# First layer's MLP: latents by a seven-product scheme, context as its own stage, rotation tables in double batches on two engines

## The chip, the cores and the metric

One core of one Trainium2 chip runs the whole program. The metric is the device time of one execution in microseconds; three runs of the kernel before took 3078.25, 3080.51 and 3085.92 us, so its time is the median, 3080.51 us. TensorE multiplies matrices into PSUM; VectorE, ScalarE and GpSimd work element by element; SyncE (SP) issues most of the DMAs, GpSimd's queue a few.

## The reference

Two layers over 1024 latent tokens and 256 context tokens of width 1024. The first layer mixes by attention, the second by a state-space model, and each ends in an MLP with hidden width 4096. Only the first layer's MLP treats the context too, since the context is not needed after the second mixer.

```
def _mlp(h, w1, w2):
    return jnp.square(jax.nn.relu(h @ w1)) @ w2

for i in range(DEPTH):                       # DEPTH = 2
    need_ctx = i < DEPTH - 1
    ...                                      # modulation, mixer
    x = x + g1 * y
    h2 = _rmsnorm(x, norm2_g[i], NORM_EPS) * (1.0 + sc2) + sh2
    x = x + g2 * _mlp(h2, mlp_w1[i], mlp_w2[i])
    if need_ctx:
        ctx = ctx + g1c * yc
        h2c = _rmsnorm(ctx, norm2_g[i], NORM_EPS) * (1.0 + sc2c) + sh2c
        ctx = ctx + g2c * _mlp(h2c, mlp_w1[i], mlp_w2[i])
return _rmsnorm(x, final_g, NORM_EPS)
```

## The kernel before

Everything is kept transposed: 128 channels on the partitions, tokens along the free axis, in blocks of 512, 512 (latents) and 256 tokens (context). Matrices are multiplied in a rounded 32-bit format, and for accuracy each operand is split into a high and a low part: a product is three matmuls, high by high, high by low and low by high (`mm3`, lines 328 to 335).

Stages follow one another: modulation and input projection; attention; output projection (`out_proj`, line 1118), which also forms the statistics and the normed, split input `Hh`, `Hl` of the MLP; the first MLP (`mlp`, line 1142); the state-space mixer (`ssm`, line 1627); its gate (`glu`); the second MLP (`mlp_s`, line 1187).

`mlp` goes through the 4096 hidden channels in 16 steps of 256. In each step one call of `weights` (line 317) brings two pages of the first matrix and another two of the second: a page of 512 KB is loaded into one of two raw buffers, ScalarE makes its high part (line 324), VectorE its low part (line 325), and the raw buffer is then free for the next page. Two buffers hold high and two hold low parts. Then come, for context and both latent blocks, 48 matmuls of the first product, relu and square (lines 1158 to 1161), 48 matmuls of the second product and the additions to the residual stream (`add_x`, line 1109). A pair of pages so serves 144 matmuls.

Between these, `prep` takes one step of a side job at a time (`work` in `build`): the second layer's modulation (`ada`, line 262: 12 chunks of 4 pages, each page multiplied by TensorE as it comes, and one transposition a chunk) and the rotation tables of the state-space mixer (`ssm_table`, line 1556): for each of 32 channel pairs, a table of 160 complex powers is doubled eight times over by complex products on GpSimd, and stored to memory.

`mlp_s` computes the second layer's MLP by Strassen's scheme: the operands are cut into 2 x 2 blocks, and seven products of block sums take the place of eight. Its eight units alternate between the first and the second matrix, each with seven products of 48 matmuls of 512 columns; sums of weight blocks are made by DMAs that add into memory, sums of inputs by VectorE. Its order is written out: every operation is given to a planner (`Plan`, line 115) with an engine, a cost and a due time, and the planner's order is then fixed for TensorE, ScalarE, VectorE and GpSimd.

Elsewhere only GpSimd keeps the order of the program; on the other engines and on SP's queue a scheduler orders by the program's order and by when it reckons an operation to be ready. Every engine, and each queue, executes its list in order: an instruction that waits holds all behind it.

After the first MLP, `u_norm` (line 1576) forms the statistics of the stream and copies it to memory for the mixer.

Of the kernel before, what the change touches and what calls it, by code (L numbers as in the profile page):

```python
# [30 lines left out]
def host_layout(inp):  # L31
# [26 lines left out]
    a["w1b"] = g["mlp_w1"][1].reshape(2, 4, P, 4, 2, 512).transpose(3, 4, 0, 2, 1, 5).reshape(4, 2, 2, P, 2048)  # L58
    a["w2b"] = g["mlp_w2"][1].reshape(4, 2, 4, P, 2, 512).transpose(0, 4, 1, 3, 2, 5).reshape(4, 2, 2, P, 2048)
# [157 lines left out]
class Net:  # L217
    def __init__(self, tc, a):
        self.tc, self.nc, self.a = tc, tc.nc, a

# [107 lines left out]
    def mm3(self, out, terms, first=True, last=True):  # L328

        nc = self.nc  # L330
        n = len(terms)
        for i, (lh, ll, rh, rl) in enumerate(terms):
            nc.tensor.matmul(out, lh, rh, start=first and i == 0, stop=False)  # L333
            nc.tensor.matmul(out, lh, rl, start=False, stop=False)  # L334
            nc.tensor.matmul(out, ll, rh, start=False, stop=last and i == n - 1)  # L335


    def rstd_steps(self, xv, n, ps, sp, then, spread=True, added=0):
# [57 lines left out]
        bc = ps.tile([P, 512], F32, name="n_bc", tag="bc", bufs=1)  # L396
# [78 lines left out]
    def in_proj(self, ps, sm, xs, pools, prep):  # L475
# [27 lines left out]
        pools()  # L503
# [614 lines left out]
    def out_proj(self, ps, sp):  # L1118
        nc, a = self.nc, self.a

        def then(b, bc):
            self.scaled(lambda ct: self.xv0(ct, b), BLK[b][1], 0, 1, int(b == 2), bc, sp, self.to_H(b))
        step = self.follow(self.xv0, ps, sp, then, added=5)
        w = {}
        for b in (2, 0, 1):
            n = BLK[b][1]

            for mp in range(4) if b else (2, 3, 0, 1):
# [4 lines left out]
                for j in range(2):  # L1133
# [5 lines left out]
                    step(b, ct)  # L1139
        step()  # L1140

    def mlp(self, i, first, xv, ps, mp, prep, last):

        nc, a = self.nc, self.a
        for f in range(16):
            w1 = self.weights(a["w1"][2 * f:2 * f + 2])
            w2 = self.weights(a["w2"][2 * f:2 * f + 2])
            hid = {}
            for b in first:
                n = BLK[b][1]  # L1150
                hh = mp.tile([P, 2, n], F32R, name="hid_h", tag=f"hh{b}", bufs=1)
                hl = mp.tile([P, 2, n], F32R, name="hid_l", tag=f"hl{b}", bufs=1)
                for j in range(2):
                    acc = ps.tile([P, 512], F32, name="m_acc", tag="mm")
                    wh, wl = (x[:, j].rearrange("p (k m) -> p k m", k=KT) for x in w1)
                    self.mm3(acc[:, :n], [(wh[:, k], wl[:, k], self.Hh[b][:, k], self.Hl[b][:, k]) for k in range(KT)])
                    r = mp.tile([P, 512], F32, name="m_r", tag="m_r", bufs=2)
                    nc.scalar.activation(r[:, :n], acc[:, :n], AF.Relu)  # L1158
                    nc.scalar.activation(hh[:, j], r[:, :n], AF.Square)  # L1159
                    nc.vector.tensor_tensor(r[:, :n], r[:, :n], r[:, :n], ALU.mult)  # L1160
                    nc.vector.tensor_tensor(hl[:, j], r[:, :n], hh[:, j].bitcast(F32), ALU.subtract)
                prep()
                hid[b] = hh, hl
            step = last() if f == 15 else lambda b, ct: ct % 4 or prep()
            for b in sorted(first):
                n = BLK[b][1]
                hh, hl = hid[b]
                for ct in range(KT):
                    acc = ps.tile([P, 512], F32, name="m_acc", tag="mm")
                    c = slice(P * ct, P * ct + P)  # L1170
                    self.mm3(acc[:, :n], [(w2[0][:, j, c], w2[1][:, j, c], hh[:, j], hl[:, j]) for j in range(2)])
                    self.add_x(xv(ct, b), acc[:, :n], self.mv(i, 5, ct, int(b == 2)))
                    step(b, ct)
        step()


# [10 lines left out]
    def mlp_s(self, mp, wp, ps):  # L1187
        nc, a = self.nc, self.a
        V, S, PE, G = nc.vector, nc.scalar, nc.tensor, nc.gpsimd

        blocks = []
        blocks += [wp.tile([P, 4, 512], F32, name=f"st_wa{j}") for j in range(2)]
        sa = [wp.tile([P, 2, 2, 512], F32R, name=f"st_a{j}") for j in range(2)]
        blocks += [wp.tile([P, 4, 512], F32, name=f"st_wb{j}") for j in range(2)]
        sb = [wp.tile([P, 2, 512], F32R, name=f"st_b{j}") for j in range(4)]

        blocks.append(self.xc.rearrange("p k s c -> p (k s c)").rearrange("p (k c) -> p k c", k=4))
        hid = {(m, n): mp.tile([P, 4, 512], F32, name=f"st_h{m}{n}") for m in range(2) for n in range(2)}

        t1, t2, t4, tt = (mp.tile([P, 4, 512], F32, name=f"st_t{x}") for x in ("1", "2", "4", "t"))  # L1200
        bank = [ps.tile([P, 4, 512], F32, name=f"st_b{i}") for i in range(2)]
        rings = dict(A=[(f"A{i}",) for i in range(5)], a=[(f"a{i}",) for i in range(2)], b=[(f"b{i}",) for i in range(4)], X0=[("X0",)], X1=[("X1",)])
# [6 lines left out]
        xv = lambda m, n, t: self.xv1(4 * m + t, n).rearrange("p s c -> p (s c)")  # L1209
        gate = lambda m, t: self.mv(1, 5, 4 * m + t, 0)  # L1210
# [634 lines left out]
def build(tc, a, probe=None):  # L1845
# [14 lines left out]
    with ExitStack() as es:  # L1860
        net.setup(es)
        with net.pool("H0") as hp, ExitStack() as ws:
# [27 lines left out]
            with net.pool("ps2", 5, space=PSUM) as ps, tc.manual_schedule(engines={mybir.EngineType.Pool}):  # L1890
                with net.pool("nrm") as sp:
                    net.out_proj(ps, sp)
                if stop("out_proj"):
                    return
# [59 lines left out]
```

## Time and profile before

| what | value |
|---|---|
| runs | 3078.25, 3080.51, 3085.92 us |
| profiled execution | 3081.73 us |
| its span | 3080.0 us |
| TensorE busy | 93% of the span |
| VectorE busy | 62% |
| ScalarE busy | 38% |
| GpSimd busy | 38% |

The profile comes from one execution of its own. The span runs from the first to the last instruction that the profile shows. Matmuls are pipelined: the duration of one overlaps the next, so the pace of a row of matmuls is the distance between their starts. PEclk is the granted clock of TensorE as a share of 2.4 GHz. "A <- B" in a tile's name reads "A is written from B".

### The profile page before, as it was taken

Reading aid. Unit: us, or ns where it says so; the run is one execution under the profiler, and the core shown is the slowest. Engines: PE = TensorE matmul, PEld = TensorE weight load, DVE = VectorE, ACT = ScalarE, POOL = GpSimd, SP = SyncE. Lnnn points to the kernel's source line nnn. Section 1 sums busy time; section 2 is a strip of 40 time slices with the busy share of each in tenths; the row PEclk is TensorE's granted clock in tenths of the full one; section 3 lists DMA queues with packets and bytes.
Section 4 is the critical chain, followed back from the end, with each engine's and each line's share of the span. In section 5 each row is a group of like instructions: output and inputs, shape, how many; then the busy total and the mean of one; then the engine's idle time right before and its main releaser. Section 6 shows DMA issues by size and latency. Waiting matters only on the chain. (4 is left out here: it accounts for less than half of the span.)

```text
span 3080.0 us, 46255 instructions
## 1 busy us (share of the span) xinstructions
PE 2878.7 (93%) x17352; PEld 2377.3 (77%) x17352; DVE 1920.8 (62%) x3337; ACT 1185.0 (38%) x2211; POOL 1160.0 (38%) x2346
## 2 busy tenths in 40 slices
PE   7999998888999999999999999967699799999997
PEld 4878887777878777787888888856588688888885
DVE  3887686988664555554554545489923566666665
ACT  3322214676663321111112121245422365656563
POOL 3343233555442277777787000167623200000001
PEclk9999999999999999999999999988899899999998
DMA  6356664233543124333311111366432444554441
GB/s 241 110 187 220 206 221 143 70 90 104 154 118 140 55 97 128 108 120 101 76 60 48 44 41 42 101 184 182 125 108 75 111 117 126 125 126 125 125 110 55
DMA packets 172305, 363.47 MB, mean 118 GB/s; under 512 B 34689, under 2 KB 97185, under 8 KB 162865
## 3 DMA queue, kind: packets, MB, share of 16 engines
q1 hardware_dynamic: 162384, 310.62, 31.5%
q0 software_dynamic: 9696, 49.90, 7.5%
q8 instruction: 136, 2.23, 0.3%
q14 instruction: 89, 0.72, 0.1%
HBM read 294.97 MB, written 65.49 MB: 117 GB/s over the span
## 5 line engine op out<-in xcount | busy, mean ns | idle before, releaser
L1316 PE MATMUL st_b<-st_b,st_a 128*128 128x512 f32 x2688 | 614.2, 391 | 10.3 <-DVE st_b L1307 7.2
L1316 PEld LDWEIGHTS st_b<-st_b,st_a 128*128 128x128 f32 x2688 | 506.7, 189 | 117.8 <-DVE st_b L1307 7.8
L324 ACT ACTIVATE w_hi<-w_raw 128x1024 fp32r<-128x1024 f32 x132 | 136.7, 1053 | 460.6 <-PE m_acc L334 351.7
L333 PE MATMUL m_acc<-hid_h,w_hi 128*128 128x512 f32 (+1 forms) x768 | 277.1, 361 | 0.0
L333 PE MATMUL m_acc<-Hh,w_hi 128*128 128x512 f32 (+1 forms) x768 | 273.9, 357 | 0.0
L334 PE MATMUL m_acc<-hid_l,w_hi 128*128 128x512 f32 (+1 forms) x768 | 272.6, 355 | 0.0
L335 PE MATMUL m_acc<-Hh,w_lo 128*128 128x512 f32 (+1 forms) x768 | 272.3, 354 | 0.0
L335 PE MATMUL m_acc<-hid_h,w_lo 128*128 128x512 f32 (+1 forms) x768 | 272.1, 354 | 0.0
L334 PE MATMUL m_acc<-Hl,w_hi 128*128 128x512 f32 (+1 forms) x768 | 272.1, 354 | 0.0
L325 DVE TENSOR_TENSOR w_lo<-w_raw,w_hi 128x1024 fp32r<-128x1024 f32 x132 | 169.3, 1294 | 155.7 <-ACT w_hi L324 148.2
L1109 DVE SCALAR_TENSOR_TENSOR xl<-m_acc,m,xl 128x512 f32<-128x512 f32 x256 | 189.5, 747 | 116.4 <-PE m_acc L335 116.1
L1160 DVE TENSOR_TENSOR m_r<-m_r 128x512 f32<-128x512 f32 (+1 forms) x96 | 60.8, 635 | 229.0 <-ACT hid_h L1159 228.8
L333 PEld LDWEIGHTS m_acc<-hid_h,w_hi 128*128 128x128 f32 x768 | 145.0, 189 | 36.0 <-issue 14.4
L333 PEld LDWEIGHTS m_acc<-Hh,w_hi 128*128 128x128 f32 x768 | 145.7, 190 | 24.4 <-issue 4.5
L334 PEld LDWEIGHTS m_acc<-hid_l,w_hi 128*128 128x128 f32 x768 | 145.1, 189 | 22.9 <-issue 3.4
L335 PEld LDWEIGHTS m_acc<-Hh,w_lo 128*128 128x128 f32 x768 | 145.7, 190 | 20.3
L335 PEld LDWEIGHTS m_acc<-hid_h,w_lo 128*128 128x128 f32 x768 | 145.1, 189 | 20.6
L334 PEld LDWEIGHTS m_acc<-Hl,w_hi 128*128 128x128 f32 x768 | 145.7, 190 | 19.2
L1158 ACT ACTIVATE m_r<-m_acc 128x512 f32<-128x512 f32 (+1 forms) x96 | 50.1, 524 | 254.9 <-PE m_acc L335 254.0
L333 PE MATMUL ip_acc<-Hh,w_hi 128*128 128x512 f32 (+1 forms) x384 | 143.1, 374 | 4.1 <-ACT Hh L471 4.1
L334 PE MATMUL ip_acc<-Hl,w_hi 128*128 128x512 f32 (+1 forms) x384 | 139.3, 363 | 1.5 <-DVE Hl L472 1.2
L335 PE MATMUL ip_acc<-Hh,w_lo 128*128 128x512 f32 (+1 forms) x384 | 138.6, 362 | 0.0
(399 smaller groups left out, 6753.7 us busy)
## 6 DMA issues: line engine op xcount, KB each, us to landing
ada_raw<-in_wada_dram SPq DMA_DIRECT2D x96, 512.0 KB, 4.2
w_raw<-in_w_dram SPq DMA_DIRECT2D x64, 512.0 KB, 4.2
s_par<-pD SPq DMA_DIRECT2D x32, 864.0 KB, 4.5
at_q<-qD SPq DMA_DIRECT2D x152, 128.0 KB, 2.7
w_raw<-in_win_dram SPq DMA_DIRECT2D x24, 512.0 KB, 4.6
pD<-tb_cs POOLq DMA_DIRECT2D x32, 320.0 KB, 2.5
pD<-sl_w SPq DMA_DIRECT2D x16, 576.0 KB, 3.4
st_wa<-in_w1b_dram SPq DMA_DIRECT2D x9, 1024.0 KB, 6.3
```

Source lines behind the costliest of these rows:

```text
L324: nc.scalar.activation(hi[:, j], r, AF.Copy)
L325: nc.vector.tensor_tensor(lo[:, j], r, hi[:, j].bitcast(F32), ALU.subtract)
L333: nc.tensor.matmul(out, lh, rh, start=first and i == 0, stop=False)
L334: nc.tensor.matmul(out, lh, rl, start=False, stop=False)
L335: nc.tensor.matmul(out, ll, rh, start=False, stop=last and i == n - 1)
L1109: nc.vector.scalar_tensor_tensor(xv, av, gate, xv, op0=ALU.mult, op1=ALU.add)
L1158: nc.scalar.activation(r[:, :n], acc[:, :n], AF.Relu)
L1160: nc.vector.tensor_tensor(r[:, :n], r[:, :n], r[:, :n], ALU.mult)
L1316: PE.matmul(bk[p][:, mt], x, y, start=(p in (1, 2, 5) and t == 0 and i == 0), stop=(t == 3 and i == 2), skip_group_check=True)
```

## The change

The first layer's latents go through `mlp_s`, which now takes its tiles as arguments; `mlp0` and `mlp1` are its two callers. The context has a stage `mlp_ctx` before it, in two halves of 2048 hidden channels: first all 16 chunks of the hidden layer, then the second product into four PSUM banks over eight pairs of pages, and the additions at the end. The weights of the first layer are thus read twice, once as pages and once as blocks. The modulation and the tables are stepped by `prep` in the output projection (24 times) and the context stage (64 times). The latents' normed input is kept unsplit (`Hr`) and made after the output projection. In `mlp_s` two input sums share one tile and are formed again in later units; the second layer has six weight buffers in place of five, and the last statistics are stepped earlier.

```
-    def mm3(self, out, terms, first=True, last=True):
+    def mm3(self, out, terms, first=True, last=True, check=True):
...
+        def scaled(b, bc, **put):
+            self.scaled(lambda ct: self.xv0(ct, b), BLK[b][1], 0, 1, int(b == 2), bc, sp, **put)
         def then(b, bc):
-            self.scaled(lambda ct: self.xv0(ct, b), BLK[b][1], 0, 1, int(b == 2), bc, sp, self.to_H(b))
+            if b == 2:
+                scaled(b, bc, put=self.to_H(b))
+            else:
+                rs[b] = bc
...
+        def norms():
+            for b in range(2):
+                scaled(b, rs[b], to=lambda ct: self.Hr[b][:, ct])
+        return norms
...
+    def mlp_ctx(self, ps, mp, prep):
...
+        for f in range(2):
+            hid = []
+            for q in range(8):
+                w1 = self.weights(a["w1"][16 * f + 2 * q:16 * f + 2 * q + 2])
                 for j in range(2):
+                    acc = ps.tile([P, 512], F32, name="c_acc", tag="mm")
                     wh, wl = (x[:, j].rearrange("p (k m) -> p k m", k=KT) for x in w1)
+                    self.mm3(acc[:, :n], [(wh[:, k], wl[:, k], H[:, k], L[:, k]) for k in range(KT)])
+                    hh, hl = (mp.tile([P, n], F32R, name=f"c_{x}", tag=f"c_{x}{2 * q + j}", bufs=1) for x in "hl")
+                    r = mp.tile([P, n], F32, name="c_r", tag="c_r", bufs=2)
+                    nc.scalar.activation(r, acc[:, :n], AF.Relu)
+                    nc.scalar.activation(hh, r, AF.Square)
+                    nc.vector.tensor_tensor(r, r, r, ALU.mult)
+                    nc.vector.tensor_tensor(hl, r, hh.bitcast(F32), ALU.subtract)
+                    hid.append((hh, hl))
+                    prep()
+            acc = [ps.tile([P, 512], F32, name="c_acc", tag="mm") for _ in range(4)]
+            for q in range(8):
+                w2 = self.weights(a["w2"][16 * f + 2 * q:16 * f + 2 * q + 2])
                 for ct in range(KT):
...
+                        ins = self.mm3(o, [(w2[0][:, j, c], w2[1][:, j, c], *hid[2 * q + j]) for j in range(2)], first=q == 0 and ct % 2 == 0, last=q == 7, check=False)
...
+                    if ct % 4 == 3:
+                        prep()
+            for ct in range(KT):
+                self.add_x(self.xv0(ct, b), acc[ct // 2][:, n * (ct % 2):n * (ct % 2) + n], self.mv(0, 5, ct, 1))
...
+                    if p == 6 and (second or u == 0):
+                        made["t1", t] = plan.add("V", 0.66, r - 14, F(tt_, V, tt[t], b12[t], b11[t], ALU.subtract), [hd(0, 1, t), hd(0, 0, t)] if second else [])
...
+                    elif p == 5 and not second and u:
+                        made["t1", t] = plan.add("V", 0.66, r - 14, F(tt_, V, tt[t], t2[:, t], b22[t], ALU.add))
+                    if p == 4:
+                        made["t4", t] = plan.add("V", 0.66, r - 13, F(tt_, V, z4[t], b21[t], z2[t], ALU.add), [made.get(("t2", t)), halves[2, t, "b"], *([] if second else [halves[5, t, "b"]])])
...
+                    for j, fn in enumerate(tail_steps[p == 4]):
+                        tail = plan.add("S", 0.6, e + 4 + 0.6 * j, fn, [*x, made["x", 4, j] if p == 4 else None, tail])
...
+    def mlp0(self, mp, ps, step, sp, banks):
+        blocks = [mp.tile([P, 4, 512], F32, name=f"st_w{j}") for j in range(4)] + [self.xc.rearrange("p k s c -> p (k s c)").rearrange("p (k c) -> p k c", k=4)]
...
+        self.mlp_s(0, self.xv0, self.Hr, blocks, sa, sb, hid, t2, tt, bank,
+                   self.tail(step))
...
-    def ssm_table(self, pair, pz):
...
+    def ssm_tables(self, pz):
+        nc, V, G = self.nc, self.nc.vector, self.nc.gpsimd
+        for b in range(16):
+            ep = pz.tile([P, 2, 2, 2, 8], F32, name="tb_ep", tag="tb_ep", bufs=2)
+            nc.sync.dma_start(ep.rearrange("p a d r n -> p a (d r n)"), self.eD[:, 2 * b:2 * b + 2].rearrange("p a d r n -> p a (d r n)"))
+            cs = pz.tile([P, 2, 2, 2, 160], F32, name="tb_cs", tag="tb_cs", bufs=1)
...
+            for q in range(8):
+                n = 1 << q
+                w = min(n, 160 - n)
+                mr, mi = (ep[:, :, :, r, q:q + 1].broadcast_to([P, 2, 2, w]) for r in range(2))
+                x, y = (cs[:, :, r, :, :w] for r in range(2))
+                for e, o, u, v, k, op in ((G, cs[:, :, 0, :, n:n + w], x, y, 0, ALU.subtract), (V, cs[:, :, 1, :, n:n + w], y, x, 1, ALU.add)):
+                    e.tensor_tensor(o, mr, u, ALU.mult)
+                    e.tensor_tensor(t[k][:, :, :, :w], mi, v, ALU.mult)
+                    e.tensor_tensor(o, o, t[k][:, :, :, :w], op)
+                if q % 2:
+                    yield
+            nc.gpsimd.dma_start(self.pD[:, 2 * b:2 * b + 2, 1088:1728], cs.rearrange("p a r d k -> p a (r d k)"))
...
+                with net.pool("nrm", side="right") as sp:
+                    norms = net.out_proj(ps, sp, prep)
+                    hs.close()
+                    hr = hs.enter_context(net.pool("hr0"))
+                    net.Hr = [hr.tile([P, KT, 512], F32, name=f"hr{b}") for b in range(2)]
+                    norms()
+                with net.pool("ctx") as mp, net.pool("nrm1", side="right") as sp:
+                    net.mlp_ctx(ps, mp, prep)
+                    for g in (ada, tables):
+                        for _ in g:
+                            pass
...
+                    step = net.u_norm(rp, sp, banks)
+                    for ct in range(KT):
+                        step(2, ct)
+                    step()
+            net.bc_bufs = 1
+            with net.pool("mlp0") as mp, net.pool("ps6", space=PSUM) as ps:
+                net.mlp0(mp, ps, step, sp, banks)
```

## Rows read from the trace of the kernel before

**Rows 1.** The page's busy times: engine, busy us, share of the span, instructions.
```profile
PE 2878.7 (93%) x17352; PEld 2377.3 (77%) x17352; DVE 1920.8 (62%) x3337; ACT 1185.0 (38%) x2211; POOL 1160.0 (38%) x2346
```

**Rows 2.** By stretch: length, busy PE, PEld, DVE, ACT, POOL; clock, DMA share, GB/s.
```profile
1060.70:2001.50 940.80, 939.67 (x5136) 776.31 (x5136) 470.93 (x708) 189.23 (x302) 503.75 (x1684) 1.00 0.25 80
2411.00:2430.30 19.30, 5.79 (x28) 3.94 (x26) 9.04 (x17) 5.79 (x9) 9.13 (x9) 0.64 0.00 0
2430.00:3047.60 617.60, 614.24 (x2696) 506.51 (x2696) 424.75 (x570) 365.17 (x578) 30.68 (x34) 0.99 0.46 116
```

**Rows 3.** Matmul groups by form: count, busy us, mean ns, idle before.
```profile
L1316 PE MATMUL st_b<-st_b,st_a 128*128 128x512 f32 x2688 | 614.2, 391 | 10.3 <-DVE st_b L1307 7.2 <-ACT st_a L1292 2.5 <-DVE st_a L1295 0.5
L333 PE MATMUL m_acc<-Hh,w_hi 128*128 128x512 f32 x512 | 200.9, 392 | 0.0
L333 PE MATMUL m_acc<-Hh,w_hi 128*128 128x256 f32 x256 | 73.0, 285 | 0.0
```

**Rows 4.** TensorE's timeline in the first MLP: start us, duration us, what.
```profile
1075.07 0.39 PE L333 MATMUL m_acc<-Hh,w_hi 128*128 128x512 f32 x1
...
1082.55 0.39 PE L333 MATMUL m_acc<-Hh,w_hi 128*128 128x512 f32 x1
...
1097.16 0.64 PE L285 MATMUL ada_acc<-ada_raw,act 128*32 128x256 f32 x8
...
1127.76 0.28 PE L333 MATMUL m_acc<-Hh,w_hi 128*128 128x256 f32 x1
...
1133.16 0.28 PE L333 MATMUL m_acc<-Hh,w_hi 128*128 128x256 f32 x1
```

**Rows 5.** SP's queue at the start of the second layer's gate.
```profile
2231.37 0.33 SPq L323 DMA_DIRECT2D w_raw<-in_glua_dram  x1
2232.57 0.33 SPq L323 DMA_DIRECT2D w_raw<-in_glub_dram  x1
2237.38 0.33 SPq L323 DMA_DIRECT2D w_raw<-in_glua_dram  x1
2239.49 0.33 SPq L323 DMA_DIRECT2D w_raw<-in_glub_dram  x1
```

**Rows 6.** VectorE's groups by form, 1060 to 2003 us.
```profile
L325 DVE TENSOR_TENSOR w_lo<-w_raw,w_hi 128x1024 fp32r<-128x1024 f32 x62 | 76.0, 1247 | 57.2 <-ACT w_hi L324 57.1
L1160 DVE TENSOR_TENSOR m_r<-m_r 128x256 f32<-128x256 f32 x32 | 13.9, 436 | 33.8 <-ACT hid_h L1159 33.8
L293 DVE TENSOR_TENSOR ada_e<-ada_e 64x512 f32<-64x512 f32 x12 | 8.4, 698 | 8.0 <-ACT ada_e L291 7.9
L447 DVE TENSOR_TENSOR rs_t<-rs_y 128x4 f32<-128x4 f32 x3 | 0.5, 160 | 1.4 <-POOL rs_y L441 1.4
```

**Rows 7.** GpSimd: the tables by stretch, groups by form, the tables' store.
```profile
1060.00:1960.00 900.00, 467.24 (x1632) 1.00 0.24 76
...
L1382 POOL TENSOR_TENSOR tb_cs<-tb_ep,tb_cs 128x2 f32<-128x2 f32 x32 | 7.7, 240 | 83.9 <-DMA tb_ep<-eD 83.9
L1384 POOL TENSOR_TENSOR tb_cs<-tb_cs,tb_t 128x128 f32<-128x128 f32 x32 | 19.6, 612 | 2.5
L1718 POOL TENSOR_TENSOR s_ab<-s_ab,s_ab 128x320 f32<-128x320 f32 x32 | 36.6, 1144 | 23.2 <-DVE s_ab L1713 22.7
...
pD<-tb_cs POOLq DMA_DIRECT2D x32, 320.0 KB, 2.5
```

**Rows 8.** Timeline of TensorE and ScalarE at three joints of stages.
```profile
1070.25 0.41 PE L333 MATMUL m_acc<-Hh,w_hi 128*128 128x256 f32 x1
...
1071.32 0.41 PE L335 MATMUL m_acc<-Hh,w_lo 128*128 128x256 f32 x1
...
2020.32 4.29 PE L1706 MATMUL s_X<-s_U,s_par 128*64 128x160 f32 x48 [5.07 <-ACT s_U L1669]
...
3058.36 2.19 ACT L367 ACTIVATE st_t<-xl 128x512 f32<-128x512 f32 x4 [2.08 <-PE st_b L352]
```

**Rows 9.** By stretch, behind a norm's broadcast; columns as in rows 2.
```profile
1069.90:1071.40 1.50, 1.50 (x9) 1.50 (x9) 1.12 (x2) 0.00 (x0) 0.33 (x1) 0.50 0.00 0
```

More of the change, by code (lines that the diff above doesn't have):

```diff
@@ L1 @@
+from contextlib import nullcontext
 from functools import partial as F
@@ L326, in weights @@
         return hi, lo
-    def mm3(self, out, terms, first=True, last=True):
-        nc = self.nc
-        n = len(terms)
+    def mm3(self, out, terms, first=True, last=True, check=True):
+        mm = F(self.nc.tensor.matmul, **({} if check else dict(skip_group_check=True)))
+        n, ins = len(terms), None
         for i, (lh, ll, rh, rl) in enumerate(terms):
-            nc.tensor.matmul(out, lh, rh, start=first and i == 0, stop=False)
-            nc.tensor.matmul(out, lh, rl, start=False, stop=False)
-            nc.tensor.matmul(out, ll, rh, start=False, stop=last and i == n - 1)
+            x = mm(out, lh, rh, start=first and i == 0, stop=False)
+            ins = ins or x
+            mm(out, lh, rl, start=False, stop=False)
+            mm(out, ll, rh, start=False, stop=last and i == n - 1)
+        return ins
     def rstd_steps(self, xv, n, ps, sp, then, spread=True, added=0):
@@ L395, in rstd_steps @@
             return
[L396 removed]
+        bc = ps.tile([P, 512], F32, name="n_bc", tag="bc", bufs=self.bc_bufs)
         for j in range(nb):
@@ L1363, in mlp_s @@
                 if last and p in (3, 4):
[L1365 to L1368 removed]
+                    x = [made["x", q, t] for q in (2, 7, 3) for t in range(4)]
+                    for j, fn in enumerate(tail_steps[p == 4]):
+                        tail = plan.add("S", 0.6, e + 4 + 0.6 * j, fn, [*x, made["x", 4, j] if p == 4 else None, tail])
             base += 28 * PK
@@ L1374, in mlp_s, with shim, tail @@
                 s["fn"]()
-            step()
-        self.plan = plan
+            tail_steps[2]()
+    def shim(self, sq, bank, **views):
+        small = {x: [self.act[:, 2 * i + j, 0:8] for j in range(2)] for i, x in enumerate(("n_v", "n_r", "rs_y", "rs_t"))}
+        return Views(None, n_sq=sq, **small, **views), bank is not None and Views(None, st=[bank[:, t] for t in range(2)], bc=[bank[:, t] for t in range(2, 4)])
+    def tail(self, step):
+        return [F(step, 1, ct) for ct in (4, 5, 6, 7, 0, 1, 2, 3)] + [F(step, 0, ct) for ct in range(4)], [F(step, 0, ct) for ct in range(4, 8)], step
@@ L1861, in build @@
         net.setup(es)
-        with net.pool("H0") as hp, ExitStack() as ws:
-            H(hp, range(3))
+        with ExitStack() as ws:
+            weight_pools(ws)
+            hc, hs = ws.enter_context(net.pool("Hc")), ws.enter_context(ExitStack())
+            hp = hs.enter_context(net.pool("H0"))
+            for x in "hl":
+                setattr(net, "H" + x, [(hc if b == 2 else hp).tile([P, KT, BLK[b][1]], F32R, name=f"H{x}{b}") for b in range(3)])
             with net.pool("ps0", 5, space=PSUM) as ps, net.pool("small", side="right") as sm:
@@ new lines, in build, with prep @@
+            rp = es.enter_context(net.pool("rms", side="right"))
+            net.bc_bufs = 2
+            with net.pool("ps2", 4, space=PSUM) as ps, tc.manual_schedule(engines={mybir.EngineType.Pool}), ExitStack() as ts:
+                ap, tp = (ts.enter_context(net.pool(x, side="right")) for x in ("ada", "tables"))
+                ada = net.ada([(1, n) for n in range(12)], ps, ap, ap, 2)
+                tables = net.ssm_tables(tp)
+                def prep():
+                    next(ada, None)
+                    next(tables, None)
+                with net.pool("nrm", side="right") as sp:
+                    norms = net.out_proj(ps, sp, prep)
+                    if stop("out_proj"):
+                        return
+                    hs.close()
[6 more added lines that the diff above has]
+                        for _ in g:
+                            pass
+                    net.ada_gain(1, 0)
+                    net.ada_gain(1, 1)
+                    sp, banks = Views(sp), Views(ps)
+                    step = net.u_norm(rp, sp, banks)
+                    for ct in range(KT):
+                        step(2, ct)
+                    step()
```

189 lines of the change are left out of this document (66 added, 123 removed).

## The prediction

> **What bounds the kernel now.** I read the page's busy times first, then the busy time by stretch, then the matmul groups by form, then the timeline at the places where a stage begins or ends. TensorE is busy 2878.7 us of a span of 3080.0 us [rows 1], and the first layer's MLP is its purest stretch: from 1060.7 to 2001.5 us, 939.67 of 940.80 us busy at a granted clock of 1.00, while VectorE works 470.93 us and ScalarE 189.23 us [rows 2]. There the time is the number of matmuls times the distance between their starts, and nothing else. Durations in the groups overlap (a 512-column matmul reads 392 ns), so I take distances: eleven triples of 512 columns between 1075.07 and 1082.55 us give 7.48 / 33 = 0.227 us each; fifteen triples of 256 columns between 1127.76 and 1133.16 us give 5.40 / 45 = 0.120 us each [rows 4]. Six groups of 512 matmuls of 512 columns and six of 256 matmuls of 256 columns (one of each in [rows 3]) are 3072 x 0.227 + 1536 x 0.120 = 697 + 184 = 881 us. The rest of the 940.8 us is mostly the modulation's 48 page steps, 0.64 us each [rows 4].
>
> **The change part by part.** The sum is made against the profiled execution: 3081.73 us, of which 3080.0 us is span. The median of the runs is 3080.51 us, 1.2 us lower.
>
> *Latents by Strassen.* The second layer's MLP multiplies matrices of the same size and needs 2688 matmuls of 512 columns [rows 3]; it stays fed, with 614.24 of 617.60 us busy [rows 2]. The first layer's latents drop from 3072 to 2688: 384 x 0.227 = **-87.0 us**. The new stage's splits, block sums by DMA and residual adds are those that lie beside the second layer's matmuls; I cost them at nothing as long as TensorE stays near 99% there. The second layer loses two kept sums and forms them again in three of its eight units, 24 VectorE operations of 0.68 us. That is 16 us on an engine with 424.75 of 617.60 us busy [rows 2], hidden behind matmuls: 0, at worst +3 where a sum comes late.
>
> *Context as a stage of its own.* Its 1536 matmuls of 256 columns remain: 0 in matmul time. What goes is cover. Before, a pair of weight pages fed 144 matmuls; now it feeds 48, which last 48 x 0.120 = 5.76 us. There are two raw buffers, and a page's buffer is reloaded only when VectorE has split it. The gate stage of the second layer shows one turn undisturbed (load, high part, low part): a load issued at 2231.37, the next into the same buffer at 2237.38 us, 6.0 us; the other buffer took 2232.57 to 2239.49, 6.9 us [rows 5]. A pair needs both buffers, so the loop gives a pair every 6.0 to 6.9 us. While modulation steps remain (37 of 61, after 24 in the output projection, so some 18 pairs with two each), TensorE itself takes 5.76 + 2 x 0.64 = 7.0 us and the loop hides. For the other 14 pairs I take 6.5 us, between the two turns: 14 x 0.74 = **+10 us**. Bounds: 0 if loads run ahead, +28 if shared transfers add another 1.3 us a pair.
>
> *Tables on two engines.* On GpSimd alone they took 467.24 us over the MLP's 900 us [rows 7], idle capacity that nobody waited for. Now sixteen double batches must fit into the output projection and the first 40 steps of the context stage, and VectorE works in the chain. A batch on GpSimd is three operations at each of eight widths of 4 to 256 elements. From 0.24 us at the smallest and 0.61 at 128 elements, and for 256 an estimate of 0.95 between that and 1.14 us at 320, these make 10 us, plus 0.6 us for the store's issue and some 3 us until its one buffer is free again (2.5 us to landing at half the bytes [rows 7]): 14 us a batch. VectorE's half is about 5.8 us, an estimate between 0.16 us at 4 and 0.44 at 256 elements [rows 6]. In the context stage ten batches want 140 us of GpSimd, and the latents' norms, moved here, 16 more operations of some 1 us; 40 steps last 40 x (2.88 + 0.64) = 141 us. GpSimd falls behind by about 15 us. VectorE runs in order, so a table operation that waits for GpSimd holds the next weight split, and TensorE waits for that: **+15 us**. Bounds: 0 if VectorE's order leaves the table operations behind the splits; +55 if VectorE idles through every GpSimd step. In that case it holds, per batch, its own work for two pairs (two splits and four hidden-block operations each, and 1.1 us of the modulation's sums), 2 x (2 x 1.25 + 4 x 0.44) + 1.1 = 9.6 us [rows 6], and the 10 us of the chain, 19.6 against the 14.1 us of four steps: +5.5 us, ten times. In the output projection 24 steps of 24 matmuls last 8 x (2.88 + 0.64) + 16 x (5.45 + 0.64) = 126 us and six batches want 84; only its context block, at 3.5 us a step, is as dense as the stage above: +3 us, 0 to +8.
>
> *Joints.* Output projection to context: before, TensorE is busy from the first microsecond (939.67 of 940.80 us from there on [rows 2]); the norms of both latent blocks (16 operations over 512 columns, some 0.7 us each by the 0.44 at 256 [rows 6]) now stand ahead of the first new splits: +2, 0 to +8. Context to latents: nothing here needs a long wait, since latents are normed long before; the first blocks are loaded into memory that the context's early hidden chunks gave back, but the new accumulators need the last adds done, and the context's statistics go through TensorE: +4. A joint where the norm itself is awaited has 5.79 us of work in 19.30 us [rows 2], so 0 to +13. Latents to state space: four residual adds instead of one stand between the last matmul and the statistics, but the copies of x leave earlier, and the second stall there, 5.07 us up to 2020.32 us, waits on them [rows 8]: +1, -3 to +4. Kernel's end: four of eight squares come off the last chain (2.19 us for four [rows 8]): -3, -5 to 0.
>
> Sum: -87 + 10 + 15 + 3 + 2 + 4 + 1 - 3 = **-55**; 3081.73 - 55 = 3026.7, less 1.2 for the median: **3025.5 us**. All bounds at their good end give 2985 us, all at their bad end 3110 us.
>
> **Rivals.** *The context stage stays TensorE-bound.* Loads and tables hide; only joints remain: -87 + 4 + 0 = 2993 to 2998 us. For it: with modulation steps TensorE's 7.0 us already exceed the turn. Against it: in the pairs of the first product VectorE's own work with tables is (9.6 + 5.8) / 2 = 7.7 us a pair.
>
> *VectorE stands locked to GpSimd.* The table term is +55 instead of +15, joints as taken: 3065.5 us. For it: the two engines exchange a result at each of eight widths. Against it: the order may place these operations where GpSimd is already done.
>
> *TensorE's clock falls in the context stage; slower than before.* Behind the broadcast of a norm, which TensorE had waited for, the 256-column matmuls from 1069.90 us ran at a granted clock of 0.50, the 1.2 GHz level [rows 9]: six starts from 1070.25 to 1071.32 us, 0.214 us apart [rows 8], against the 0.120 us at 2.4 GHz. If a wait in every pair kept the stage at the low level, 1536 x 0.094 = +145 us in place of the loop's 10: 3160 us. It decides from about 45% of the stage at that level: without the loop's 10 the sum is -65, of 145 us. Against it: that stretch lasted 1.5 us, and the stage's granted clock is 1.00 all the same [rows 2]. The Trainium skill's page "TensorE: Matmul & The Clock Gate", section "HAM oscillation — how this bites in real kernels", says that a matmul loop whose compute per tile is shorter than the wait for the next tile starts every tile cold. By that rule the stage would cost this rival's price; the trace agrees on the fall after a wait, but no row of this kernel shows it at every tile. My waits of under 1 us a pair are shorter than the 5.76 us of work, which is why the chance stays small.
>
> *No gain at all*: stalls of 78 to 96 us, the sum of bad ends of several terms.
>
> **How the numbers follow.** Forecast, 2998 to 3050 us: 0.62. TensorE-bound, below 2998: 0.13. Locked, 3050 to 3071: 0.13. Within 0.3% (about what a measurement can tell from no change), 3071 to 3090: 0.05. Slower, above: 0.07. Range 2993 to 3062 us. Faster 0.88, same 0.05, slower 0.07.
>
> **What would show it.** Right: 2688 first-layer Strassen matmuls 0.227 us apart, some 610 us; a context stage of 230 to 250 us where 208 us (1536 x 0.120 and 37 steps of 0.64) would be all busy; its TensorE gaps ended by VectorE's low parts, and VectorE's table operations waiting for GpSimd. Wrong: a context stage at 208 us (first rival), near 280 us with VectorE waiting on GpSimd in each batch (second), a granted clock near 0.5 there (third), or idle TensorE in the Strassen stage because a block sum or a residual add comes late, which I have costed at nothing.

## The result: slower, and the profile after

The changed kernel takes 3127.19 us (median of four runs, 3124.43 to 3129.51) against 3082.38 us: ratio 1.0146, 95% interval 1.0128 to 1.0163. I had forecast 3025.5 us, at most 3062. In its page (as [rows 1]) TensorE works 51 us less, and the span is 44 us longer:

```profile
span 3123.8 us, 45656 instructions
PE 2827.6 (91%) x16968; PEld 2335.8 (75%) x16968; DVE 2147.7 (69%) x3849; ACT 1464.3 (47%) x2643; POOL 887.6 (28%) x1129
```

The busy times by stretch, columns as in [rows 2]: output projection, context, the joint between context and latents, latents by Strassen, joint to the state-space stage.

```profile
936.00:1092.80 156.80, 138.49 (x785) 105.91 (x784) 91.25 (x224) 32.66 (x51) 81.68 (x171) 0.95 0.55 165
1092.80:1388.40 295.60, 246.87 (x1831) 219.50 (x1827) 202.58 (x438) 95.53 (x141) 149.48 (x286) 0.90 0.58 197
1388.40:1396.80 8.40, 2.69 (x26) 1.51 (x25) 2.38 (x8) 3.46 (x9) 3.33 (x3) 0.70 0.72 134
1396.80:2015.70 618.90, 615.37 (x2700) 507.07 (x2704) 439.36 (x595) 367.53 (x582) 26.78 (x31) 0.99 0.47 117
2015.70:2053.10 37.40, 8.66 (x57) 3.62 (x54) 5.94 (x18) 9.52 (x19) 9.05 (x10) 0.55 0.79 243
```

The Strassen stage is as pure as hoped. The losses are the context stage, 295.6 us where 233 stood in my sum, at a clock of 0.90; the output projection; and the last joint, 37.4 us where the trace of before has 9.4 (last matmul of the MLP 2001.51, first state-space matmul 2010.87). Before, then after:

```profile
2001.51 0.28 PE L335 MATMUL m_acc<-hid_h,w_lo 128*128 128x256 f32 x1
2010.87 2.56 PE L1706 MATMUL s_X<-s_U,s_par 128*64 128x160 f32 x18 [3.91 <-DMA s_par<-pD]
```

```profile
2053.06 5.04 PE L1754 MATMUL s_X<-s_U,s_par 128*64 128x160 f32 x48 [18.25 <-ACT s_U L1717]
```

What TensorE, and then VectorE and GpSimd, waited for in the context stage (us in total, times, longest):

```profile
PE c_acc L338 <- DVE w_lo L327: 31.4, 17, 4.9
PE c_acc L335 <- ACT w_hi L326: 8.0, 8, 2.6
```

```profile
DVE w_lo L327 <- ACT w_hi L326: 28.8, 20, 3.2
DVE tb_cs L1606 <- POOL tb_cs L1605: 19.7, 3, 6.9
DVE tb_cs L1606 <- DMA pD<-tb_cs: 17.8, 6, 6.4
POOL tb_cs L1605 <- DMA pD<-tb_cs: 49.8, 10, 7.5
```

One such wait in the timeline (start, duration, what, idle before and what ended it):

```profile
1176.80 0.75 POOL L1618 DMA_DIRECT2D pD<-tb_cs  x1 [1.56 <-DVE c_r L1176]
1181.73 0.10 POOL L1605 MEMSET tb_cs<- 128x4 f32 x1 [4.18 <-DMA pD<-tb_cs]
1181.80 0.06 DVE L1606 MEMSET tb_cs<- 128x4 f32 x1 [3.59 <-DMA pD<-tb_cs]
1182.67 1.25 DVE L327 TENSOR_TENSOR w_lo<-w_raw,w_hi 128x1024 fp32r<-128x1024 f32 x1
1183.97 0.58 PE L338 MATMUL c_acc<-c_h,w_lo 128*128 128x256 f32 x1 [2.94 <-DVE w_lo L327]
```

GpSimd waits 1.56 us for VectorE's half before it can issue the batch's store; the store holds the one buffer for 4.9 us from its issue; the next batch's first fill stands at the head of VectorE's list and waits for that; the weight split behind it waits too, and TensorE for the split.

The last joint, VectorE and then SP's queue. The last product ends at 2015.7, and its four residual adds (L1340) start at 2020.70, behind the other block's statistics. SP's first load goes out at 2034.92, after the last reader of the tile that L1650 writes, whose memory it takes over; so the copies of x behind it come late, and the state-space matmuls start at 2053:

```profile
2018.59 0.16 DVE L393 TENSOR_SCALAR act<-st_b 128x4 f32<-128x4 f32 x1 [10.54 <-PE st_b L391]
2020.70 2.72 DVE L1340 SCALAR_TENSOR_TENSOR xl<-st_b,m,xl 128x512 f32<-128x512 f32 x4
2034.03 0.29 DVE L1650 TENSOR_TENSOR st_tt<-act,u_mask 128x128 f32<-128x128 f32 x1
2051.68 1.70 DVE L1710 TENSOR_TENSOR s_U<-s_U,rU 128x320 f32<-128x320 f32 x4 [17.36 <-DMA s_U<-xS]
```

```profile
2034.92 0.33 SPq L1733 DMA_DIRECT2D s_par<-pD  x1
2035.34 5.14 SPq L1722 DMA_DIRECT2D s_T<-KD  x8
2041.64 6.79 SPq L1706 DMA_DIRECT2D s_U<-xS  x8
```

### The profile page after: what moved, and what is told of

Same layout as the page of the kernel before. It is cut to its first block, busy times and chain, and to the rows that moved or that the text cites. A ratio compares the mean times of both kernels' runs of the same rounds, so it can differ in the third digit from the quotient of the medians.

```text
span 3123.8 us, 45656 instructions
## 1 busy us (share of the span) xinstructions
PE 2827.6 (91%) x16968; PEld 2335.8 (75%) x16968; DVE 2147.7 (69%) x3849; ACT 1464.3 (47%) x2643; POOL 887.6 (28%) x1129
## 5 line engine op out<-in xcount | busy, mean ns | idle before, releaser
L1315 PE MATMUL st_b<-st_b,st_a 128*128 128x512 f32 x5376 | 1228.4, 391 | 18.1 <-DVE st_b L1306 10.3
L1315 PEld LDWEIGHTS st_b<-st_b,st_a 128*128 128x128 f32 x5376 | 1013.3, 189 | 233.3 <-DVE st_b L1306 11.3
L1340 DVE SCALAR_TENSOR_TENSOR xl<-st_b,m,xl 128x512 f32<-128x512 f32 x224 | 157.4, 744 | 61.0 <-PE st_b L1315 61.0
L1303 ACT ACTIVATE st_b<-st_h 128x512 fp32r<-128x512 f32 x192 | 118.8, 626 | 86.8 <-PE st_b L1315 81.6
L1294 DVE TENSOR_TENSOR st_a<-st_w,st_a 128x1024 fp32r<-128x1024 f32 x90 | 109.9, 1222 | 64.3 <-ACT st_a L1291 64.3
L1306 DVE TENSOR_TENSOR st_b<-st_h,st_b 128x512 fp32r<-128x512 f32 x192 | 127.5, 684 | 20.7 <-ACT st_b L1303 19.8
L753 PE MATMUL at_sc<-at_k,at_q 128*128 128x256 f32 (+2 forms) x608 | 125.1, 336 | 9.9 <-ACT at_p L843 4.4
L1343 ACT ACTIVATE st_h<-st_h 128x512 f32<-128x512 f32 x224 | 120.2, 622 | 0.2
L761 PE MATMUL at_bank<-ident,at_p 128*128 128x128 f32 (+1 forms) x680 | 102.3, 279 | 7.1 <-ACT at_aT L770 3.4
L335 PE MATMUL g_acc<-Hh,w_hi 128*128 128x512 f32 x256 | 100.7, 393 | 3.1 <-ACT w_hi L326 3.1
```

The lines of the kernel that those rows point to most:

```text
L335: x = mm(out, lh, rh, start=first and i == 0, stop=False)
L753: PE.matmul(sc[:, c:c + n], qd["q"][:, m, hl, qo:qo + P], k["k"][m][:, k0:k0 + n], start=(hl == 0), stop=(hl == 1))
L1303: S.activation(sl["b", t][:, 0], x, AF.Copy)
L1306: V.tensor_tensor(sl["b", t][:, 1], x, sl["b", t][:, 0].bitcast(F32), ALU.subtract)
L1315: PE.matmul(bk[p][:, mt], x, y, start=(p in (1, 2, 5) and t == 0 and i == 0), stop=(t == 3 and i == 2), skip_group_check=True)
L1340: V.scalar_tensor_tensor(x, bk[p][:, t].rearrange("p (s c) -> p s c", s=x.shape[1]), g, x, op0=ALU.mult, op1=ALU.add)
```

## Experiments

Ratios are to the kernel before, in the same chip session; differences in us are between medians. Each edit is made to the changed kernel unless it says otherwise.

**Without the tables' arithmetic.**

```
-            (fills, and six operations at each of eight widths on two engines)
...
+            G.memset(cs, 1.0)
+            for _ in range(4):
+                yield
```

> Leaves out the arithmetic of the rotation tables: a batch is one fill on GpSimd and the store, and VectorE gets no table operation; the rest is the changed kernel. Theory T (the tables stand in VectorE's in-order list ahead of the weight splits): the context stage falls from 295.7 us to 220 to 245, the output projection from 156.8 us to 135 to 145, the time from 3127 to 3040 to 3070 us. Rival L (two raw buffers and the shared load queue set the pace): the context stage stays above 270 us and the time above 3090 us.

3055.93 us, ratio 0.9914 (0.9892 to 0.9935): 71 us less. Output projection and context stage:

```profile
940.30:1085.20 144.90, 137.60 (x786) 105.74 (x784) 51.05 (x80) 33.34 (x53) 31.62 (x32) 0.95 0.61 184
1085.20:1317.50 232.30, 219.93 (x1832) 198.29 (x1832) 128.97 (x183) 94.06 (x140) 35.77 (x40) 0.99 0.72 247
```

Theory T holds: the tables on two engines cost 71 us. The context stage is 63 us shorter: 27 us less busy TensorE for the same matmuls (clock 0.99 instead of 0.90) and 36 us less idle (12.4 instead of 48.7).

**Each half by itself.** VectorE's half, or GpSimd's, on data of its own. Two more things differ from the changed kernel: the small loads of the exponents (`tb_ep`, the 64 numbers a partition by which a batch is multiplied up) go out on GpSimd's queue, and the store sends a constant tile, so that no batch waits for a store.

```
-            nc.sync.dma_start(ep.rearrange(...
+            nc.gpsimd.dma_start(ep.rearrange(...
...
-                for e, o, u, v, k, op in ((G, ...), (V, ...)):
+                o, u = cs[:, :, :, n:n + w], cs[:, :, :, :w]
+                E.tensor_tensor(o, mr, u, ALU.mult)
+                E.tensor_tensor(t[:, :, :, :w], mi, u, ALU.mult)
+                E.tensor_tensor(o, o, t[:, :, :, :w], ALU.add)
...
-            nc.gpsimd.dma_start(self.pD[:, 2 * b:2 * b + 2, 1088:1728], cs.rearrange("p a r d k -> p a (r d k)"))
+            G.dma_start(self.pD[:, 2 * b:2 * b + 2, 1088:1728], out)
```

> Of the tables only VectorE's half is left, on data of its own (GpSimd's half is left out, and the store sends a constant tile; the exponents' loads are on GpSimd's queue): VectorE does as many operations of the same sizes as in the changed kernel, but waits for no result of GpSimd and for no store. Theory X (the price of the tables is the exchange with GpSimd, step by step, and the two engines slowing each other): at most 15 us above the kernel without table arithmetic, 3056 to 3071 us. Theory O (VectorE's own 16 x 6 us of work between the weight splits is the price): 3090 to 3111 us.

> The other half: only GpSimd's operations are left, on data of their own, and VectorE has no table operation. What is above 3055.9 us is what GpSimd's work costs by slowing VectorE's splits. Theory X, second form (the engines slow each other): 15 to 35 us more, 3071 to 3091. Otherwise at most 10 us more, 3056 to 3066.

3058.75 us (0.9934, 0.9920 to 0.9949) and 3058.68 us (0.9936, 0.9917 to 0.9955): each half costs some 3 us by the medians and 6 to 7 by the ratios, within the spread of the runs; the context stage itself is 243.2 and 237.8 us long, against 232.3 without tables. The 71 us can't be set beside these as they stand, since they contain the exponents' loads on SP's queue. With these loads on GpSimd's queue both halves together cost 54 us (3110.30 us, below). So most of the price comes only when both engines work on one chain, as theory X has it. The table operations alone in the context stage of the changed kernel and of the one with VectorE's half (VectorE's busy time first):

```profile
1092.80:1388.40 295.60, 75.19 (x255) 133.36 (x267) 0.90 0.58 197
```

```profile
1081.40:1324.60 243.20, 50.87 (x249) 0.96 0.70 237
```

The same operations take 75.2 us where both engines work, 50.9 alone (a 256-element sum 726 against 423 ns); the waits in front of them, 41 us (19.7 and 17.8 above, and 3.3 in single steps), do not exist alone. So a chain that needs 51 us of VectorE's list holds it for 116. No run had both halves at work without the exchange and the store, so how much comes from the engines slowing each other (24 us more of busy time) and how much from the waits is not told apart.

**What part is a queue's.** A second buffer for the batch, for which one buffer of exponents instead of two and narrower temporaries make room; the exponents' loads on GpSimd's queue; both.

```
-            ep = pz.tile([P, 2, 2, 2, 8], F32, name="tb_ep", tag="tb_ep", bufs=2)
+            ep = pz.tile([P, 2, 2, 2, 8], F32, name="tb_ep", tag="tb_ep", bufs=1)
...
-            cs = pz.tile([P, 2, 2, 2, 160], F32, name="tb_cs", tag="tb_cs", bufs=1)
+            cs = pz.tile([P, 2, 2, 2, 160], F32, name="tb_cs", tag="tb_cs", bufs=2)
...
-            nc.sync.dma_start(ep.rearrange(...
+            nc.gpsimd.dma_start(ep.rearrange(...
```

> A second buffer for a table batch, so that the next batch need not wait for the store of the last (the two temporaries 128 instead of 160 wide and one buffer of exponents instead of two make room). If the wait for the store is what holds VectorE (theory T, first form): its waits for the store, 12.7 us in the output projection and 17.8 us in the context stage, go and the time falls by 20 to 45 us, to 3082 to 3107. If it is the step by step exchange between the two engines (theory T, second form): within 10 us of 3127.

> Only the small loads of the exponents (one per table batch) go from SP's queue to GpSimd's; the tables stay on both engines. Theory S (such a load waits in SP's in-order queue until the batch two before it is done with its buffer, and holds the weight loads behind it): the time falls by 15 to 35 us, to 3092 to 3112. Theory T (VectorE's own order and GpSimd's pace hold the splits): within 8 us of 3127, since VectorE still waits for GpSimd at the same places.

> Both small edits together: a second table buffer (alone 11 us less than the changed kernel) and the exponents' loads on GpSimd's queue (alone 17 us less). Theory T (most of the 71 us that the tables cost is VectorE's own table operations between its weight splits, waiting step by step for GpSimd): about 3099 us, and not below 3090. Rival S (store and exponents' loads are all of it, each hiding behind the other when only one is removed): 3060 to 3080 us.

3116.14 us (1.0112, 1.0097 to 1.0127), 3110.30 us (1.0098, 1.0081 to 1.0115) and 3111.18 us (1.0097, 1.0082 to 1.0112): 11, 17 and 16 us less than the changed kernel. The second buffer misses its expected 20, but its 11 us are net of a loss: with one buffer of exponents SP's queue stood 53.7 us at their loads, 28.9 in the changed kernel. Both together fit neither theory and gain no more than the queue alone, while the one buffer of exponents brings a wait of its own, on GpSimd and on VectorE (context stage):

```profile
POOL tb_cs L1613 <- DMA tb_ep<-eD: 50.5, 10, 6.6
```

```profile
DVE tb_cs L1613 <- DMA tb_ep<-eD: 17.4, 7, 3.3
```

SP's queue is some 17 of the 71 us. The other 54 I could not split further.

**All table operations on GpSimd**, first with the exponents' loads left on SP's queue, then on GpSimd's.

```
-            V.memset(cs[:, :, 1, :, 0:1], 0.0)
+            G.memset(cs[:, :, 1, :, 0:1], 0.0)
...
-                ..., (V, cs[:, :, 1, :, n:n + w], y, x, 1, ALU.add)):
+                ..., (G, cs[:, :, 1, :, n:n + w], y, x, 1, ALU.add)):
```

> Double batches as in the changed kernel, but all six operations of a width on GpSimd. Theory T: VectorE's splits wait for no table, so the two stages come out within 15 us of those without tables, 3045 to 3085 us; GpSimd needs some 340 us for 16 batches and ends close to the end of the context stage. Rival P (the two engines slow each other whenever both work, whatever the order): GpSimd now works all the time beside VectorE, VectorE's low parts stay at 1.27 us or more, and the context stage stays above 270 us, 3090 us or more. Rival L: no change of the stage, 3110 us or more.

> All table operations on GpSimd and the exponents' loads on GpSimd's queue: neither VectorE's list nor SP's queue holds anything of the tables. Theory S for the loss of the earlier run with all operations on GpSimd (3224.8 us): that loss goes, the context stage falls from 372 us to 230 to 250, the time to 3050 to 3080. Rival (GpSimd at work slows VectorE, or its late statistics hold the stages): still above 3100 us.

3224.80 us (1.0464, 1.0447 to 1.0482): a clear miss. VectorE waits for no table, and yet the context stage takes 372.6 us. SP's queue tells why (what it waited for in the context stage, and its timeline):

```profile
SPq L1602 <- POOL tb_t L1614: 163.2, 9, 25.7
```

```profile
1245.32 0.33 SPq L1602 DMA_DIRECT2D tb_ep<-eD  x1
...
1246.70 0.85 SPq L325 DMA_DIRECT2D w_raw<-in_w_dram  x2
1272.36 0.33 SPq L1602 DMA_DIRECT2D tb_ep<-eD  x1
```

From 1247.6 to 1272.4 the queue stands still: the load of the exponents waits for GpSimd to leave its buffer, and the weights behind it starve. Moved to GpSimd's queue: 3140.62 us (1.0190, 1.0175 to 1.0205). The context stage is now 242.8 us, as expected, but the time is not, and the rival holds; the next bound is at the stage's end, where a small operation of the context's statistics stands behind GpSimd's backlog of tables:

```profile
PE u_r L1654 <- DVE u_lm L1650: 63.1, 1, 63.1
```

```profile
DVE rs_t L451 <- POOL rs_y L445: 61.9, 1, 61.9
```

**The modulation's pages**, four buffers instead of two, without table arithmetic.

> As the kernel without table arithmetic (3055.9 us), with four buffers instead of two for the pages of the modulation, so that its loads stand less long in SP's queue before TensorE has read the page that was in the buffer. If these loads are what keeps the context stage at 232 us instead of 208, and the output projection at 143.7 instead of 134: 15 to 30 us less, 3026 to 3041. If two raw buffers and VectorE's split set the pace: within 8 us of 3055.9.

3055.84 us (0.9917, 0.9902 to 0.9931): no difference. Those loads do not set the rest.

**The same tables in the kernel before**, on two engines, in its MLP where a pair of pages feeds 144 matmuls.

```
-                        for p in range(32):
-                            net.ssm_table(p, tp)
-                            for _ in range(3):
...
+                        for _ in net.ssm_tables(tp):
...
```

> The kernel before, with nothing changed but the tables: double batches on VectorE and GpSimd with the exponents' loads on SP's queue, stepped with the modulation in its MLP (temporaries 128 wide and one buffer of exponents, for room). Theory C (the same table work costs nothing where a pair of pages feeds 144 matmuls and costs 71 us where it feeds 48): within 8 us of the kernel before. Rival (tables on two engines cost this much wherever they stand, since they slow both engines): 3100 us or more.

3156.94 us, ratio 1.0249 (1.0231 to 1.0266): 76 us slower. My theory of lost cover falls. While the tables run, and after:

```profile
1060.00:1460.00 400.00, 346.54 (x1877) 272.52 (x1874) 269.65 (x654) 65.74 (x106) 181.37 (x425) 0.92 0.32 105
1460.00:1960.00 500.00, 500.00 (x2667) 424.97 (x2666) 247.20 (x368) 93.25 (x145) 0.00 (x0) 1.00 0.17 49
```

TensorE there waits not for weights but for VectorE's sums and adds (`ada_e` 22.7 us, `xl` 12.9, `m` 12.5), which stand behind table operations: VectorE waited 31.4 us for stores and 16.8 us for GpSimd's fill. (SP also stood 123.7 us at exponents, of which there was one buffer.) So on two engines the tables cost as much in this MLP as in the context stage, while on GpSimd alone TensorE was busy there for 939.67 of 940.80 us [rows 2].

**The joint to the state-space stage.**

```
-            lm = sp.tile([P, P], F32, name="u_lm", tag="u_lm", bufs=1).rearrange(...)
+            lm = own.rearrange("p (b w) -> p b w", b=nb)
...
-            for k in list(live):
+            for k in [b] if (b, ct) in hold else list(live):
...
-        s, b = self.shim([t2[:, t] for t in range(4)], bank[0], u_lm=...)
+        s, b = self.shim([t2 ...] + [hid[0, 0][:, t] for t in range(4)], bank[0], n_e=...)
```

A first form had the four square buffers of the changed kernel (a square then overwrites the second block's sum before it is read, so that block's scaling is another number):

> Only the joint from the latents' MLP to the state-space stage: the small tile of the last statistics gets memory of its own, and the second block's statistics are not taken further until the four last residual adds are done. Theory J (the adds stand behind a statistics chain in VectorE's list, and the loads behind one that waits for that tile's memory): last product to first state-space product falls from 37.5 us to 14 to 22 us, the time by 15 to 23 us, to 3104 to 3112. Rival: the 24 small loads of that stage, issued after the last matmul, take as long anyway: less than 6 us gained.

> The joint of the latents' MLP and the state-space stage alone: the last statistics' small tile with memory of its own, the second block's statistics taken further only behind the four last residual adds, and eight square buffers instead of four with two of their own for the sums (from hidden tiles that are read no more). Theory J: last product to first state-space product falls from 37.5 us to 17 to 23 us, the time by 14 to 22 us, to 3105 to 3113. Rival (the loads issued after the last product set it): less than 6 us gained.

3115.26 us (1.0106, 1.0081 to 1.0130) with a joint of 24.4 us, a little short of what was expected, then 3110.77 us (1.0099, 1.0084 to 1.0114) with 23.0 us: 16 us less. Theory J holds, though order and memory were changed together; the adds now start with the last product's end:

```profile
2015.09 2.73 DVE L1340 SCALAR_TENSOR_TENSOR xl<-st_b,m,xl 128x512 f32<-128x512 f32 x4 [7.64 <-PE st_b L1315]
```

**Versions that do all the work**, with the joint's edit and the tables on GpSimd alone: in eight batches of four pairs; all in the Strassen stage; six batches in the context stage and ten in the Strassen stage.

```
+        for j in range(n):
+            plan.add("G", 1.3, 30 + 530.0 * j / n, F(next, side, None))
...
-        sa = [self.wp.tile([P, 2, 1024], F32R, name="st_a", tag="wh")...
+        sa = [x[2].rearrange(...) for x in (self.Hh, self.Hl)]
```

> Nothing is left out. Tables on GpSimd alone in 8 batches of four pairs (fewer small operations: some 33 us a batch by the durations of the earlier runs, 264 us in all), the exponents' loads on GpSimd's queue, stepped in two of three steps of the output projection and three of four of the context stage, so that GpSimd is done before the context's statistics need it; and the joint to the state-space stage as in the joint's own run. If the causes are the table operations in VectorE's list, the exponents' loads in SP's queue, and the joint's order: 3055.9 (no table arithmetic) less 16 for the joint, plus up to 15 where GpSimd holds a statistic: 3040 to 3055 us. If GpSimd is still behind at the end of the context stage, as with all operations of double batches: 3065 us or more.

3070.86 us (0.9969, 0.9954 to 0.9984), a miss. TensorE waits at no result of GpSimd, but the context stage takes 268 us. VectorE's operations by form in it:

```profile
L327 DVE TENSOR_TENSOR w_lo<-w_raw,w_hi 128x1024 fp32r<-128x1024 f32 x62 | 89.1, 1438 | 81.8 <-ACT w_hi L326 80.2 <-PE ada_acc L287 0.8 <-DVE ada_e L295 0.4
L1176 DVE TENSOR_TENSOR c_r<-c_r 128x256 f32<-128x256 f32 x32 | 23.2, 728 | 7.1 <-ACT c_h L1175 6.9
L1112 DVE SCALAR_TENSOR_TENSOR xc<-c_acc,m,xc 128x256 f32<-128x256 f32 x14 | 6.1, 477 | 2.9 <-PE c_acc L338 2.9
```

Without table arithmetic these take 1224, 418 and 473 ns: larger GpSimd operations beside them stretch those with two operands in SBUF, and not the add with one operand in PSUM. That this stretch is what lengthens the stage is not shown. The Trainium skill's page "SBUF — State Buffer", section "Who interferes with whom", says that a VectorE instruction with two SBUF inputs contends with a GpSimd instruction that reads SBUF; the trace agrees, with these numbers.

> Nothing is left out. All 16 double batches on GpSimd alone, one operation at a time spread over the latents' Strassen stage (its high weight sums move into the context's input tiles, which are read no more, and the tables into their place), and the joint to the state-space stage as in the joint's own run. If a stage that TensorE bounds hides them, as the MLP of the kernel before did: the Strassen stage stays at 619 us, and the time is that without table arithmetic less the joint's 16: 3036 to 3050 us. If GpSimd slows VectorE's block sums or delays the block sums by DMA that GpSimd's queue issues: the stage takes 635 us or more and the time is 3060 us or more.

3055.90 us (0.9928, 0.9910 to 0.9945): the context stage is 227.8 us, the Strassen stage 640.7, as long as the second theory had it; the time lies between the two. GpSimd, whose queue also issues the sums of weight blocks, waited 59.7 us for exponents there.

> Nothing is left out. As with all tables in the Strassen stage, but six of the 16 batches on GpSimd in the context stage (half the work of both halves cost under 4 us there), ten in the Strassen stage from its second unit on, and each batch's exponents are loaded one batch ahead, so that GpSimd does not wait for them in front of the block sums that its queue issues. If those waits (59.7 us on GpSimd in the Strassen stage) made that stage 640.7 us long instead of 619: 622 to 630 us there, a context stage of 230 to 240 us, and 3040 to 3052 us in all. If GpSimd's slowing of VectorE made it long: 3052 us or more.

3044.42 us, ratio 0.9893 (0.9869 to 0.9917). The context and the Strassen stage:

```profile
1074.50:1315.70 241.20, 221.84 (x1832) 200.31 (x1831) 143.01 (x183) 94.14 (x140) 162.87 (x332) 0.97 0.66 226
1323.80:1943.10 619.30, 615.65 (x2700) 507.18 (x2704) 467.11 (x595) 367.37 (x582) 291.66 (x536) 0.99 0.51 133
```

Ten batches are hidden in 619.3 us, better than expected; whether the exponents' early load or the smaller share did it is not told apart, since both were changed. The six batches left in the context stage cost 9 us there (241.2 against 232.3). It is the fastest version of this study by its median; its interval just touches that of the version before it.

## Why the prediction was wrong

By the terms of the sum, in profiled executions:

| stage | in the sum | after | without tables |
|---|---|---|---|
| output projection and joint | 139.5 | 156.8 | 144.9 |
| context stage | 233 | 295.6 | 232.3 |
| joint | 4 | 8.4 | 8.4 |
| latents by Strassen | 630 | 618.9 | 618.8 |
| joint to the state-space stage | 10.4 | 37.4 | 37.6 |

(The first column comes from the sum so. Output projection: 119.1, from 941.7 to 1060.8 in the trace of before, with 24 x 0.64 and 5. Context stage: 208 and 25. Joint: 4. Strassen: what is left of 1059.8 - 53, the time from 941.7 to 2001.5 less what the sum takes off up to there. Last joint: 9.4 and 1.) Together the stages came out 100 us longer than the sum, and the profiled execution 99 (3125.62 for 3026.7). All bad ends together are 3113 us, with the second layer's +3 that the 3110 left out; the kernel was slower even than that.

**The failed step: the tables, +15 and +3 for a measured 71.** "GpSimd falls behind by about 15 us" priced the pace of one engine and took VectorE's list as held only by that. The nearest rival ("VectorE stands locked to GpSimd", 3065.5 us) had a price near the measured one, +55 for 63 in the context stage, but in part by luck: the waits at every step, on which that price rested, came to 3.3 us in all. What held VectorE were the starts of batches, 37.5 us for GpSimd's fill and for the last batch's store, and its own operations, which took half as long again beside GpSimd's (75.2 against 50.9 us). The store stood in my sum, but only in GpSimd's pace, at 3 us; in the context stage GpSimd waited 49.8 us for ten of them. The exponents' loads, moved to SP's queue, were not priced at all, some 17 us. With those on GpSimd's queue the context stage takes 280.6 us with both halves, 243.2 and 237.8 with one, 242.8 with all operations on GpSimd, and 232.3 with none: some 32 of the 48 us come only with the chain on both engines, its exchange and its store.

**Second: latents to state space, +1 for a measured +28.** "Four residual adds instead of one" counted the adds and not their place: VectorE's list has them behind the other block's statistics, and SP's queue has its loads behind the last statistics' tile. The bounds, -3 to +4, came from stalls of before, where neither holds. 14 of the 28 us went when order and memory were changed; the other 14 remain and are open.

**Right:** Strassen's products. The stage took 618.9 us, near the "some 610" and 11 less than the sum left for it. The context stage without tables took 232.3 us where 218 stood, and not for the loop of loads: of the 24 us above an all-busy 208, TensorE waited 5.8 for weight parts and 6.6 for other things, and was busy 219.9 us instead of 208. The output projection was 8 us longer than the sum even without tables; neither rest was traced further. The joint of context and latents took 4 us more, and the kernel's end gained nothing.

**The third rival** (a falling clock; 3160 us) came in part: not at 0.50, but 0.90 over the stage, as a follower of the waits: 27 of the 63 us. I had taken "waits of under 1 us a pair"; the rows above show up to 4.9 us.

## What to carry to other kernels

A dependent chain split over two in-order engines costs what it holds in both lists, not its operations: here a few us for each half alone and 54 for both, with the small loads out of the way, 71 with them. Before moving a side job, look for what stands behind each of its instructions, its small loads on a shared queue included; a job on one idle engine, in a stage that another engine bounds, and stepped in small pieces, cost nothing in the last version here (619.3 us), but 22 us while more of it stood there and its small loads came late (640.7). At the end of a stage, ask not how many operations are left but which one stands in front of them.

## What the runs showed of the hardware

- GpSimd operations beside VectorE stretch those with two SBUF operands, and more where they are larger: the low part 1224 ns without tables, 1309 with double batches on GpSimd, 1438 with batches of four pairs, GpSimd being busy 82% and 81% of the stage in the last two; the add from PSUM 473 to 477 ns in all. The 128x256 product does not follow so cleanly: 418, 498 and 728 ns, but 603 beside GpSimd's half alone. The low parts without tables and with double batches on GpSimd:

```profile
L327 DVE TENSOR_TENSOR w_lo<-w_raw,w_hi 128x1024 fp32r<-128x1024 f32 x62 | 75.8, 1224 | 87.8 <-ACT w_hi L326 87.5
```

```profile
L327 DVE TENSOR_TENSOR w_lo<-w_raw,w_hi 128x1024 fp32r<-128x1024 f32 x62 | 81.2, 1309 | 81.2 <-ACT w_hi L326 80.6 <-DVE ada_e L296 0.2
```

- With 17 waits for low parts, of up to 4.9 us, over 32 pairs of pages the mean granted clock of the context stage was 0.90, between its two levels of 2.4 GHz (1.00) and 1.2 GHz (0.50); with 7 waits of up to 0.8 us, 4 us in all, it was 0.99 for the same matmuls. Without tables:

```profile
PE c_acc L338 <- DVE w_lo L327: 4.0, 7, 0.8
```
